# Products by halves: when the next down weights are loaded and cast, which low parts VectorE makes, and one piece of VectorE's order in the second feed-forward stage

## The chip, the cores and the metric

The kernel runs on one core of a Trainium2 chip. The metric is the device time of one execution in microseconds (us). A difference of about 0.5% (4.1 us here) is the least that a measurement of this kernel tells from no change.

## The reference

One encoder layer on 512 tokens of width 1024, all in float32: a feed-forward half-step, a mixer (Fourier groups beside grouped-query attention), a second feed-forward half-step, and a last norm.

```python
for _ in range(DEPTH):                                   # DEPTH = 1
    x = x + 0.5 * swiglu(rms_norm(x, ffn1_norm), ffn1_w_gate, ffn1_w_up, ffn1_w_down)
    h = rms_norm(x, mix_norm)
    u = h @ w_in
    ...
    x = x + jnp.concatenate([f_out, a_out], axis=-1) @ w_out
    x = x + 0.5 * swiglu(rms_norm(x, ffn2_norm), ffn2_w_gate, ffn2_w_up, ffn2_w_down)
return rms_norm(x, final_norm)

def swiglu(h, w_gate, w_up, w_down):
    return (jax.nn.silu(h @ w_gate) * (h @ w_up)) @ w_down
```

The feed-forward width is 2752: 21 blocks of 128 columns and a tail of 64. The change touches the two feed-forward stages alone.

## The kernel before

**Precision.** Each float32 operand of a product is split into a high part (a cast to fp32r, made by ScalarE) and a low part (source minus high part). A product is three TensorE passes: high by high, high by low, low by high. The low part is made in one of two ways: by a VectorE subtraction (`lows`, line 140), or by `rest_by_dma` (lines 169 and 170): ScalarE writes minus the high part into the place of the low part (an ACTIVATE), and GpSimd starts a DMA that adds the source to it.

**Stages.** Stage 1 (the first feed-forward, 0 to 330 us of the profile), the mixer (330 to 484 us), stage 2 (the second feed-forward, 484 us to the end). `ffn` makes both feed-forward stages.

**Groups.** Within a stage the 21 blocks j of the hidden width come in four groups. Stage 1: blocks 0, the tail "t", 1 and 2; then 3 to 8; 9 to 14; 15 to 20. Stage 2: blocks 0, "t" and 1; then 2 to 7; 8 to 13; 14 to 20. For each group the kernel multiplies the group's hidden activations by the group's part of the down weights: eight output tiles dn_0 to dn_7, each 128 by 512, three passes for each block of the group (18 matmuls for a group of six). The result of dn_d is added to the residual `gx` by VectorE (line 629). The first group's gate and up products are plain; the last of its plain pairs (block 2) is evacuated by `evacuate`, run from `rest()`.

**Products by halves.** The gate and up products of all later blocks are made by `seven`: the pair (gate, up) of a block is one 2 by 2 block product in seven half-size products instead of eight. One block takes one period of seven products, P0 to P5 and P9, of eight matmuls each. While group g's down products are made, the pairs for the next group are not yet under way: `seven` runs ahead of the down products of its group, over the blocks of that group but shifted by one (for the group 3 to 8 it makes blocks 4 to 9, six periods; the last loop of stage 1 makes 16 to 20, of stage 2 15 to 20). The last block's P9 and what hangs on it (the names in `LATE`) come after dn_0, by `rest()`.

**The order in a period** is written out in `TABLE`: names that end in h are ScalarE casts of weights, in l the low parts (a for the raw weights a11 and a12, s and t for their sums, d for a22), c1 to c4 the VectorE sums, f, g, p, l, u, v, si, mu, h the evacuation (pA: ScalarE copies half of bank q; pB, lA, lB, uA, uB: VectorE adds), nh or l the low part of the activation. A + or - moves a name to the next or the last block. ScalarE, VectorE and GpSimd follow this order inside `seven`; TensorE and SyncE follow the order of the program's text throughout; in the rest of `ffn` a list scheduler orders the other engines, with `issue_after` edges (`behind`) that put an instruction behind an anchor on the same engine.

**The places that the change touches.** `load_below()` starts the transfers of the raw down weights for dn_0 and dn_1 (`raw_tile`, line 164, on SyncE's queue). `below()` casts them (line 182) and makes their low parts (line 140); the two calls hang on the names in `BELOW`, at a block beyond the last. Raw down weights and raw up weights share three buffers ("raw"), so that a transfer starts when an earlier tile's last reader is done. A down weight's high and low part take two of the four shared slots of `ring`; dn_2 gets dn_0's slots, dn_3 gets dn_1's. In the last period of a group the low part of the last block's activation is made by VectorE, all others by `rest_by_dma`.

**What else a reader needs.** The first product of a period, P0, multiplies a11, whose low part is made by `rest_by_dma` (BY_DMA), so the transfer written `ring<-raw_g` has to land before P0's second matmul (line 452).

Of the kernel before, what the change touches and what calls it, by code (L numbers as in the profile page):

```python
# [12 lines left out]
ALU = mybir.AluOpType  # L13
# [26 lines left out]
PLACES = 7  # L40
HALF = S // 2
USES = "a11", "a12", "s2", "s1", "s4", "s3", "a22"
BELOW = 'a.h', 'd.h'
HELD = 2
FIRST = ("ld", "a.h", "a.l", "c1", "d.h", "d.l", "c2", "c3", "c4", "s.h", "s.l", "t.h", "t.l")
TABLE = """
# [47 lines left out]
def asf(ap):  # L94
    return ap.bitcast(F32)
# [3 lines left out]
def encoder(ctx, tc, A, out):  # L99
    nc = tc.nc  # L100
# [36 lines left out]
            f(*a)  # L137

    def lows(lo, src, hi):
        nc.vector.tensor_tensor(out=lo, in0=src, in1=asf(hi), op=ALU.subtract)  # L140

    def slot_at(tile, i, rooms=0):
        o = i * KD * P + rooms * ROOM
# [150 lines left out]
    def ffn(norm, after, wgu, wd, wdt, groups, opening, closing):  # L294
# [4 lines left out]
        n_ = norm.n  # L299
        n_plain = len(groups[0])  # L300
        with tc.tile_pool(name=f"act{n_}", bufs=1) as ap, tc.tile_pool(name=f"sums{n_}", bufs=2) as sp:
            room(ap, 128)
            acts = ap.tile([P, PLACES * 2 * S + ROOM], F32R, name=f"at{n_}")
            at = acts[:, FRONT + LOWER : FRONT + LOWER + PLACES * 2 * S].rearrange("p (n a b) -> p n a b", a=2, b=S)
# [5 lines left out]
            def place(j):  # L310
                where[j] = free.pop(0)
                return where[j]
# [8 lines left out]
            def gate(c, between={}, by_dma=False):  # L321
                with ExitStack() as behind:
                    for i in (norm.squared, norm.added) if n_ and c else ():
                        behind.enter_context(tc.issue_after(i.ins))
                    whi, wlo = weights(wgu[c], f"gu{n_}_{c}", by_dma=by_dma)
                ps = bank(f"gu{n_}_{c}")
                for k in range(KD):
                    between.get(k, int)()
                    product(ps, whi[:, k, :], wlo[:, k, :], hh[k], hl[k], k == 0, k == KD - 1, turn=True)
                return ps  # L330
# [38 lines left out]
            def back(ts):  # L369
                plain[:] = [t for t in plain if all(t is not q for q in ts)]  # L370
# [67 lines left out]
            anchors = {}  # L438

            def seven(js, first, finish, load_below, below):  # L440
# [86 lines left out]
                def do(i, name):  # L527
                    shift = name.count("+") - name.count("-")
                    name = name.rstrip("+-")
                    i += shift  # L530
                    if i == len(js) - 2 and name == "P3":
                        load_below()
                    if i == len(js) and name in BELOW:
                        below()
                    if i not in range(len(js)):
                        return
                    o = state.setdefault(i, {})
                    if "w" not in o:
                        o.update(prepare(js[i]))
                    if "P0" not in o:  # L540
                        o.update(evacuation(js[i], o))
                    if i and (i, name) != (1, "ld") or not i and name not in FIRST:
                        o["l" if name == "nh" and i == len(js) - 1 else name]()
                    if i == 0 and name == "P0":
                        finish()

# [12 lines left out]
            def down_raw(d, group, gi):  # L559

                js = [j for j in group if j != "t"]
                return raw_tile(wd[d][:, js[0] : js[-1] + 1, :], f"dn{n_}_{d}_{gi}", len(js))

            def down(d, group, gi):

                js = [j for j in group if j != "t"]
                src, halves_ = wd[d][:, js[0] : js[-1] + 1, :], closing and gi == len(groups) - 1 and d >= KD - LAST
                raw = raws[d] = loads.pop(0) if loads else down_raw(d, group, gi)
                whi, wlo = weights(src, "", len(js), raw, skip=SKIP if halves_ else 0)
                if halves_:  # L570
                    token_weights(d, js)
                w = wt[d // 4][:, d % 4 * P : (d % 4 + 1) * P]

                def steps(ps, t):
                    for i, j in enumerate(group):
                        h, l = (at[:, where[j], o, t] for o in range(2))
                        first, last = i == 0, i == len(group) - 1
                        turn = t == every
                        if j == "t":
                            o, h, l = (turned(p) if turn else p for p in (ps[:, t], h, l))  # L580
                            nc.tensor.matmul(o, w, h, start=first, stop=False)
                            nc.tensor.matmul(o, w, l, start=False, stop=last)
                        else:
                            k = j - js[0]
                            cut = first and d == KD - LAST and t == slice(0, HALF)
                            product(ps[:, t], whi[:, k, :], wlo[:, k, :], h, l, first, last, cut, turn)
                        yield

                return steps
# [44 lines left out]
            for gi, group in enumerate(groups):  # L634
                last = gi == len(groups) - 1
                ahead = []
                if gi:
                    downs, loads = [], []
                    rest = seven(
                        range(group[0] + 1, min(group[-1] + 2, NF)), ready, finish,  # L640
                        lambda: loads.extend(down_raw(d, group, gi) for d in range(2)),
                        lambda: downs.append(down(len(downs), group, gi)),
                    )
                else:
                    downs, loads = [], []
                    lent = [acts[:, FRONT + i * KD * P : FRONT + (i + 1) * KD * P] for i in range(PLACES - 4, PLACES)]
                    plain.extend(lent)
                    row = []
                    pss = dict(enumerate(opening(gate, lambda: norm.column([norm.acc]), lambda: row.append(norm.row()))))
                    back(lent[:2])  # L650
                    due, parts, left = [*pss, "t"], list(range(KH)), range(2 * len(pss), 2 * n_plain)
                    pss["t"] = [gate(2 * NF)]
                    tail_weights()
                    for i, c in enumerate(left):
                        pss.setdefault(c // 2, []).append(gate(c, by_dma=i in (1,) if n_ else i > 0))
                        if due:
                            j = due.pop(0)
                            evacuate(at[:, place(j)], n_, pss[j], norm)
                        if c % 2 and c != left[-1]:
                            due.append(c // 2)  # L660
                        while len(parts) * len(left) > (len(left) - 1 - i) * KH:
                            o = parts.pop(0)
                            operands(row[0], o, o + 1)

                    def rest():
                        evacuate(at[:, place(n_plain - 1)], n_, pss[n_plain - 1], norm)

                def added(d, ps):
                    residual(d, ps, every)
# [6 lines left out]
                for d in range(KD):  # L676
# [19 lines left out]
                    if d == 0:  # L696
                        rest()
                        if last:

                            lent = slots[KD - 2 : KD]  # L700
                            plain[0:0] = lent
                            continue
                    def finish(waiting=waiting, added=added if last or d < KD - 1 else lambda d, ps: residual(d, ps, every)):
                        for d_, ps, steps in waiting:
                            for _ in steps:
                                pass
                            added(d_, ps)
# [10 lines left out]
    def evacuate(at, n_, pss, norm):  # L718
        g = tp.tile([P, S], F32, tag="g", name=f"g{n_}p")
        u = tp.tile([P, S], F32, tag="u", name=f"u{n_}p")  # L720
        h, l = at[:, 0], at[:, 1]
        if len(pss) == 2:
            nc.vector.tensor_tensor(out=g, in0=pss[0], in1=norm.rb, op=ALU.mult)
            nc.vector.tensor_tensor(out=u, in0=pss[1], in1=norm.rb, op=ALU.mult)
            nc.scalar.activation(g, g, AF.Silu)
            nc.vector.tensor_tensor(out=u, in0=g, in1=u, op=ALU.mult)
            nc.scalar.copy(h, u)
            lows(l, u, h)
        else:

            o, p = slice(FT, P), slice(0, FT)
            nc.vector.tensor_tensor(out=u, in0=pss[0], in1=norm.rb, op=ALU.mult)
            nc.scalar.activation(g[o], u[p], AF.Silu)
            nc.vector.tensor_tensor(out=u[o], in0=g[o], in1=u[o], op=ALU.mult)
            nc.scalar.copy(h[o], u[o])
            nc.scalar.copy(h[p], u[o])
            lows(l[o], u[o], h[o])
            nc.scalar.copy(l[p], asf(l[o]))
# [909 lines left out]
```

## Time and profile before

| what | us |
|---|---|
| median of 3 runs | 822.95 (819.89 to 823.01) |
| the profiled execution's own time | 820.42 |
| its span, first to last instruction | 818.6 |
| TensorE busy with matmuls | 807.9 (99%) |
| VectorE, ScalarE, GpSimd busy | 639.8, 548.6, 83.5 |
| mean granted TensorE clock | 0.999 |

Rows of the timeline give start, length, engine, line, operation, out<-in (buffer numbers left out) and shapes; in brackets stands the engine's idle time ahead of the instruction and what ended it. SPq is SyncE's queue, PEld TensorE's weight load. A matmul's length holds its way through the array, so a stall is read from starts: back to back, matmuls of 512 columns start 0.22 us apart, and a pair of 512 and 256 columns takes 0.33 us. Rows of the DMA view give the transfers issued in a window: KB each and the time to landing. Rows of the waits view give the total, the number and the longest.

### The profile page before, as it was taken

To read this page: it belongs to the slowest core of one execution; us is meant where nothing else is said; L and a number is where in the kernel's file an instruction comes from. 1 tells how busy PE (TensorE), PEld (TensorE's weight loads), DVE (VectorE), ACT (ScalarE), POOL (GpSimd) and SP (SyncE) were. 2 spreads that over 40 slices of the span, in tenths; PEclk is the share of its full clock that TensorE was granted. 3 is DMA by queue.
4 is the path that set the end of the run, shared out by engine and by line. 5 is a ranking of instruction groups with operands and counts; after the bars stand their busy time and mean duration, and the time that the engine had idled before them with its cause. 6 is when DMAs were issued, how large, how long until landed. Compare 5 with 4: busy or idle time off the path is not lost.

```text
span 818.6 us, 11867 instructions
## 1 busy us (share of the span) xinstructions
PE 807.9 (99%) x4376; PEld 705.8 (86%) x4376; DVE 639.8 (78%) x1071; ACT 548.6 (67%) x876; POOL 83.5 (10%) x95
## 2 busy tenths in 40 slices
PE   9999999999999999999999999999999999999997
PEld 7888988898888888889988888889888988888886
DVE  7996998388856967799998588989874998389673
ACT  7774885278725845779999558568733875278562
POOL 0120210011100100211000001102100110011001
PEclk9999999999999999999999999999999999999999
DMA  7775885559644743352110325668653785459422
GB/s 258 178 166 158 192 208 135 147 141 215 141 160 96 175 102 116 104 174 78 52 53 26 103 67 146 150 199 202 170 141 103 182 208 135 151 130 216 97 77 104
DMA packets 40779, 115.82 MB, mean 141 GB/s; under 512 B 4752, under 2 KB 10256, under 8 KB 40720
## 3 DMA queue, kind: packets, MB, share of 16 engines
q1 hardware_dynamic: 27776, 82.61, 33.0%
q0 software_dynamic: 12224, 31.47, 20.7%
q10 hardware_dynamic: 720, 0.98, 0.3%
q8 instruction: 34, 0.56, 0.3%
q14 instruction: 25, 0.20, 0.1%
HBM read 84.24 MB, written 2.10 MB: 105 GB/s over the span
## 4 chain that ended last, share of the span: by engine, by line
PE 85%; DMA 9%; DVE 4%; issue 1%; ACT 1%; POOLq 0%; POOL 0%; DVEq 0%; ACTq 0%
PE dn L196 25%; PE r L449 12%; PE mix L196 9%; DMA ring<-raw_g 7%; PE r L452 7%; PE gu L196 3%; PE c L449 3%; PE p L449 3%; PE q L449 3%; PE gu L804 3%; PE mix L1304 2%; PE mix L1264 2%; PE c L452 2%; PE p L452 2%; PE q L452 2%
## 5 line engine op out<-in xcount | busy, mean ns | idle before, releaser
L196 PE MATMUL dn<-at,ring 128*128 128x512 f32 x900 | 203.4, 380 | 0.0
L196 PEld LDWEIGHTS dn<-at,ring 128*128 128x128 f32 x900 | 167.7, 188 | 29.0 <-DVE ring L140 0.2
L449 PE MATMUL r<-rt,ring 128*128 128x512 f32 x560 | 191.4, 383 | 0.0
L452 PE MATMUL r<-rt,ring 128*128 128x256 f32 x560 | 153.7, 274 | 3.2 <-DMA ring<-raw_g 3.2
L449 PEld LDWEIGHTS r<-rt,ring 128*128 128x128 f32 x560 | 105.1, 188 | 18.7
L452 PEld LDWEIGHTS r<-rt,ring 128*128 128x128 f32 x560 | 105.2, 188 | 5.5 <-DMA ring<-raw_g 5.1
L629 DVE SCALAR_TENSOR_TENSOR gx<-dn,gx 128x512 f32<-128x512 f32 x61 | 41.9, 690 | 76.4 <-PE dn L196 76.3
L182 ACT CAST ring<-raw_dn 128x768 fp32r<-128x768 f32 (+3 forms) x58 | 45.2, 783 | 67.0 <-PE dn L196 48.5
L140 DVE TENSOR_TENSOR ring<-s,ring 128x1024 fp32r<-128x1024 f32 x70 | 85.1, 1220 | 2.5 <-ACT ring L404 0.5
L404 ACT CAST ring<-s 128x1024 fp32r<-128x1024 f32 x70 | 72.6, 1043 | 6.0 <-PE p L449 5.6
L140 DVE TENSOR_TENSOR ring<-raw_dn,ring 128x768 fp32r<-128x768 f32 (+3 forms) x58 | 51.6, 893 | 6.2 <-issue 4.1
L170 POOL DMA_DIRECT2D ring<-raw_g x35 | 30.0, 858 | 249.1 <-ACT ring L169 179.5
L169 ACT ACTIVATE ring<-ring 128x1024 fp32r<-128x1024 f32 x38 | 40.3, 1060 | 13.6 <-PE dn L196 12.5
L196 PE MATMUL gu<-ring 128*128 128x512 f32 x216 | 48.9, 381 | 0.0
L449 PE MATMUL c<-rt,ring 128*128 128x512 f32 x140 | 48.6, 383 | 0.0
L449 PE MATMUL p<-rt,ring 128*128 128x512 f32 x140 | 48.5, 383 | 0.0
L449 PE MATMUL q<-rt,ring 128*128 128x512 f32 x140 | 48.4, 382 | 0.0
L485 ACT COPY p<-r 128x512 f32<-128x512 f32 x35 | 19.9, 570 | 41.9 <-PE r L452 41.9
L196 PEld LDWEIGHTS gu<-ring 128*128 128x128 f32 x216 | 40.4, 188 | 6.9
L170 POOL DMA_DIRECT2D at<-u x29 | 24.9, 858 | 200.1 <-ACT p L505 192.0
L404 ACT CAST ring<-raw_g 128x1024 fp32r<-128x1024 f32 x35 | 36.8, 1051 | 11.9 <-DMA raw_g<-in_wgu 11.9
L452 PE MATMUL c<-rt,ring 128*128 128x256 f32 x140 | 38.4, 274 | 0.0
(282 smaller groups left out, 1704.8 us busy)
## 6 DMA issues: line engine op xcount, KB each, us to landing
raw_g<-in_wgu SPq DMA_DIRECT2D x35, 512.0 KB, 4.2
raw_u<-in_wgu SPq DMA_DIRECT2D x35, 512.0 KB, 5.4
ring<-raw_g POOLq DMA_DIRECT2D x35, 512.0 KB, 7.6
raw_dn<-in_wd SPq DMA_DIRECT2D x40, 384.0 KB, 3.3
at<-u POOLq DMA_DIRECT2D x29, 256.0 KB, 3.8
raw_gu<-in_wgu SPq DMA_DIRECT2D x12, 512.0 KB, 3.8
raw_o<-in_wo SPq DMA_DIRECT2D x8, 512.0 KB, 3.4
raw_dn<-in_wd SPq DMA_DIRECT2D x8, 448.0 KB, 3.7
```

The source lines that it names most:

```text
L140: nc.vector.tensor_tensor(out=lo, in0=src, in1=asf(hi), op=ALU.subtract)
L169: nc.scalar.activation(lo, asf(hi), AF.Copy, scale=-1.0)
L170: nc.gpsimd.dma_start(out=lo, in_=src, accum_op=ALU.add)
L182: nc.scalar.copy(hi[:, :n, :], raw[:, :n, :])
L196: nc.tensor.matmul(ps, a, b, start=first and b is mhi and a is whi, stop=last and a is wlo)
L404: nc.scalar.copy(hi, src())
L449: nc.tensor.matmul(turned(ps), whi[:, ks], turned(m), start=first and i == 0, stop=False, skip_group_check=True)
L452: nc.tensor.matmul(turned(ps[:, :HALF]), wlo[:, ks], turned(m[:, :HALF]), start=False, stop=i == KH - 1, skip_group_check=True,)
L485: nc.scalar.copy(o[key], o["r"])
L629: nc.vector.scalar_tensor_tensor(out=x[d][:, t], in0=ps[:, t], scalar=0.5, in1=x[d][:, t], op0=ALU.mult, op1=ALU.add)
L804: nc.tensor.matmul(turned(pss[c]), w[:, k % 2, c], turned(m[k]), start=k == 0 and m is hh and w is hi, stop=k == KD - 1 and w is lo,)
L1264: nc.tensor.transpose(pts[n][:, c * P : (c + 1) * P], prob[t, b, c][:, kc * P : (kc + 1) * P], ident)
```

## The change

Four edits, none of which alters what is computed.

1. `load_below()` is called at P0 of a loop's last block, no longer at P3 of the block before.
2. `below()` hangs on "c3" and "t.h", no longer on "a.h" and "d.h": dn_0's cast and low part move behind pA of the last period, dn_1's to where a further period's t.h would stand, behind the last block's Silu.
3. In the last group of a stage, the low part of the last block but one is made by VectorE too (the others of that group stay with the DMA). One ScalarE ACTIVATE and one GpSimd DMA go, one VectorE subtraction of 128 by 512 comes, in each stage.
4. In stage 2 the subtraction at the end of the last plain pair's evacuation becomes the VectorE anchor: what `behind` emits from then on (the down weights' low parts and the sums c1 to c4 of the first pair by halves, block 3) stands behind it on VectorE.

```diff
-BELOW = 'a.h', 'd.h'
+BELOW = "t.h", "c3"
...
     def lows(lo, src, hi):
-        nc.vector.tensor_tensor(out=lo, in0=src, in1=asf(hi), op=ALU.subtract)
+        return nc.vector.tensor_tensor(out=lo, in0=src, in1=asf(hi), op=ALU.subtract)
...
-                    if i == len(js) - 2 and name == "P3":
+                    if i == len(js) - 1 and name == "P0":
                         load_below()
                     if i == len(js) and name in BELOW:
                         below()
...
-                        o["l" if name == "nh" and i == len(js) - 1 else name]()
+                        o["l" if name == "nh" and i >= len(js) - 1 - last else name]()
...
                     def rest():
-                        evacuate(at[:, place(n_plain - 1)], n_, pss[n_plain - 1], norm)
+                        done = evacuate(at[:, place(n_plain - 1)], n_, pss[n_plain - 1], norm)
+                        if n_:
+                            anchors["DVE"] = done
...
-            lows(l, u, h)
+            return lows(l, u, h)
```

TensorE's list of instructions is the same, row by row. Three places where instructions stand differently, or where one might expect them to:

**SyncE's queue at the end of the loop over blocks 4 to 9 (stage 1).** raw_g and raw_u are a block's raw weights, raw_dn_d those of dn_d; in brackets stand the semaphores that are waited for. Before:

```order
L393 DMA raw_g_9_1047<-in_wgu 128x1024 [waits DMASW1_49,DMAHW1_49,DVE_49,Activation_49]
L393 DMA raw_u_9_1048<-in_wgu 128x1024 [waits DMAHW0_49]
L164 DMA raw_dn_0_1_1146<-in_wd 128x768 [waits DMAHW2_49,Activation_49]
L164 DMA raw_dn_1_1_1148<-in_wd 128x768 [waits DMAHW4_49,DVE_49,Activation_49]
L393 DMA raw_g_10_1332<-in_wgu 128x1024 [waits DMAHW3_49,DMASW3_49,DVE_49]
L393 DMA raw_u_10_1333<-in_wgu 128x1024 [waits DMAHW6_49,DVE_49,Activation_49]
L164 DMA raw_dn_2_1_1337<-in_wd 128x768 [waits DMAHW7_49,DVE_49]
```

The same place with the change:

```order
L393 DMA raw_g_9_1047<-in_wgu 128x1024 [waits DMASW1_49,DMAHW1_49,DVE_49,Activation_49]
L393 DMA raw_u_9_1048<-in_wgu 128x1024 [waits DMAHW0_49]
L164 DMA raw_dn_0_1_1185<-in_wd 128x768 [waits DMAHW2_49,Activation_49]
L164 DMA raw_dn_1_1_1187<-in_wd 128x768 [waits DMAHW4_49,DVE_49,Activation_49]
L393 DMA raw_g_10_1332<-in_wgu 128x1024 [waits DMAHW3_49,DMASW3_49,DVE_49]
L393 DMA raw_u_10_1333<-in_wgu 128x1024 [waits DMAHW6_49,DVE_49,Activation_49]
L164 DMA raw_dn_2_1_1337<-in_wd 128x768 [waits DMAHW7_49,DVE_49]
```

Nothing moved: between the two places of the call no other transfer is issued on SyncE's queue, and the transfers for dn_0 and dn_1 wait for the same readers of the same buffers (the cast of block 7's and of block 8's raw up weights).

**VectorE at the end of the same loop.** The names are those of `TABLE`'s tiles: s the sums and their low parts, g, p, u the evacuation's tiles of the block numbered. Before:

```order
L140 TENSOR_TENSOR ring<-raw_dn_0_1_1146,ring 128x768
L140 TENSOR_TENSOR ring<-s_0_9_1116,ring 128x1024
L459 TENSOR_TENSOR u_8_1185<-u_8_1185,r_8_1090 128x256
L140 TENSOR_TENSOR ring<-raw_dn_1_1_1148,ring 128x768
L514 TENSOR_TENSOR u_8_1185<-g_8_1139,u_8_1185 128x512
L140 TENSOR_TENSOR ring<-s_0_9_1172,ring 128x1024
L459 TENSOR_TENSOR g_9_1235<-g_9_1235,p_9_1201 128x256
L459 TENSOR_TENSOR p_9_1261<-p_9_1261,q_9_1242 128x256
L459 TENSOR_TENSOR g_9_1235<-c_9_1237,p_9_1261 128x256
```

With the change, from the second-last of these on:

```order
L459 TENSOR_TENSOR g_9_1231<-g_9_1231,p_9_1199 128x256
L140 TENSOR_TENSOR ring<-raw_dn_0_1_1185,ring 128x768
L459 TENSOR_TENSOR p_9_1257<-p_9_1257,q_9_1238 128x256
L459 TENSOR_TENSOR g_9_1231<-c_9_1233,p_9_1257 128x256
L459 TENSOR_TENSOR u_9_1271<-r_9_1189,p_9_1257 128x256
L459 TENSOR_TENSOR u_9_1271<-u_9_1271,r_9_1189 128x256
L459 TENSOR_TENSOR g_9_1231<-g_9_1231,c_9_1233 128x256
L419 TENSOR_TENSOR s_0_10_1411<-raw_u_10_1333 128x512
L140 TENSOR_TENSOR ring<-raw_u_10_1333,ring 128x512
L419 TENSOR_TENSOR s_0_10_1481<-raw_g_10_1332,raw_u_10_1333 128x512
L419 TENSOR_TENSOR s_0_10_1411<-s_0_10_1411,raw_g_10_1332 128x512
L140 TENSOR_TENSOR ring<-raw_dn_1_1_1187,ring 128x768
```

dn_0's low part now stands between gB and pB of the last block, dn_1's behind three more adds and four instructions for block 10. ScalarE at that place, with the change (before, raw_dn_0 and raw_dn_1 stood ahead of the two casts of s_0_9, nine rows further up):

```order
L505 COPY p_9_1257<-q_9_1238 128x256
L182 CAST ring<-raw_dn_0_1_1185 128x768
L404 CAST ring<-raw_g_10_1332 128x1024
L404 CAST ring<-raw_u_10_1333 128x512
L169 ACTIVATE ring<-ring 128x1024
L509 ACTIVATE g_9_1231<-g_9_1231 128x512
L182 CAST ring<-raw_dn_1_1_1187 128x768
L182 CAST ring<-raw_dn_2_1_1337 128x768
```

dn_0's cast is the first thing behind pA, dn_1's follows the last block's Silu (g_9), and dn_2's cast keeps its place behind them.

**VectorE at the opening of stage 2**, behind the first residual (u2p is block 2's activation, s_2_3 the sums of block 3). Before:

```order
L629 SCALAR_TENSOR_TENSOR gx<-dn_0_0_4917,gx 128x512
L140 TENSOR_TENSOR ring<-raw_dn_3_0_4948,ring 128x256
L419 TENSOR_TENSOR s_2_3_5024<-raw_u_3_4976 128x512
L419 TENSOR_TENSOR s_2_3_5043<-raw_g_3_4975,raw_u_3_4976 128x512
L140 TENSOR_TENSOR at_4612<-u2p,at_4612 128x512
L140 TENSOR_TENSOR ring<-raw_u_3_4976,ring 128x512
L419 TENSOR_TENSOR s_2_3_5024<-s_2_3_5024,raw_g_3_4975 128x512
L629 SCALAR_TENSOR_TENSOR gx<-dn_1_0_4947,gx 128x512
L140 TENSOR_TENSOR at_4612<-raw_dn_4_0_4962,at_4612 128x256
```

With the change:

```order
L629 SCALAR_TENSOR_TENSOR gx<-dn_0_0_4916,gx 128x512
L140 TENSOR_TENSOR at_4611<-u2p,at_4611 128x512
L140 TENSOR_TENSOR ring<-raw_dn_3_0_4947,ring 128x256
L419 TENSOR_TENSOR s_2_3_5023<-raw_u_3_4975 128x512
L419 TENSOR_TENSOR s_2_3_5042<-raw_g_3_4974,raw_u_3_4975 128x512
L140 TENSOR_TENSOR ring<-raw_u_3_4975,ring 128x512
L629 SCALAR_TENSOR_TENSOR gx<-dn_1_0_4946,gx 128x512
L140 TENSOR_TENSOR at_4611<-raw_dn_4_0_4961,at_4611 128x256
L419 TENSOR_TENSOR s_2_3_5023<-s_2_3_5023,raw_g_3_4974 128x512
```

The subtraction for u2p moved up by three rows, and the low part of dn_4 now has one block-3 sum fewer ahead of it (c2 follows it). Further down, the low part of dn_7 likewise moved ahead of block 3's last low part.

## The prediction

> **What bounds the kernel now.** I read the page's busy shares first, then the waits, then the timeline at each wait, TensorE first. The page's first part and the rows of the waits view for TensorE's two sides:
>
> ```profile
> PE 807.9 (99%) x4376; PEld 705.8 (86%) x4376; DVE 639.8 (78%) x1071; ACT 548.6 (67%) x876; POOL 83.5 (10%) x95
> PE r L452 <- DMA ring<-raw_g: 3.2, 6, 1.2
> PE dn L196 <- DVE at L140: 0.5, 1, 0.5
> PEld r L452 <- DMA ring<-raw_g: 5.1, 6, 1.5
> ```
>
> TensorE is the bound: of a span of 818.6 us it is idle for 818.6 - 807.9 = 10.7. No edit takes a matmul away, so the change can only win part of that, and it can lose wherever it makes TensorE wait anew. The named waits are two kinds: six at P0's second matmul, on the DMA that makes a11's low part (one before the last loop period of each of six loops; 3.2 us as TensorE's own idle time, 5.1 by its weight load), and one of 0.5 on VectorE at a down product. The first kind, in stage 1's first loop:
>
> ```profile
> 109.57 0.39 PE L449 MATMUL r<-rt,ring 128*128 128x512 f32 x1
> ...
> 110.12 0.38 PE L452 MATMUL r<-rt,ring 128*128 128x256 f32 x1 [0.16 <-DMA ring<-raw_g]
> ...
> 100.73 0.46 SPq L393 DMA_DIRECT2D raw_u<-in_wgu  x1
> 100.80 0.86 POOL L170 DMA_DIRECT2D ring<-raw_g  x1 [1.45 <-ACT ring L169]
> ...
> 101.30 0.37 SPq L164 DMA_DIRECT2D raw_dn<-in_wd  x1
> ```
>
> Starts 109.57 to 110.12 are 0.55 apart where a matmul of 512 columns takes 0.22: 0.33 lost. Within 0.6 us the accumulating DMA, a raw_u and a raw_dn start together. The DMA view of narrow windows shows how long each takes: first the accumulating DMA a period earlier (issued at 91.47), then the two issued at 100.80 and 101.30, then the raw_dn of another group's end (189.54), then raw_dn issued into quieter stretches (121.66 and 132.41):
>
> ```profile
> ring<-raw_g POOLq DMA_DIRECT2D x1, 512.0 KB, 7.7
> ring<-raw_g POOLq DMA_DIRECT2D x1, 512.0 KB, 9.3
> raw_dn<-in_wd SPq DMA_DIRECT2D x1, 384.0 KB, 8.9
> raw_dn<-in_wd SPq DMA_DIRECT2D x1, 384.0 KB, 10.0
> raw_dn<-in_wd SPq DMA_DIRECT2D x1, 384.0 KB, 3.2
> raw_dn<-in_wd SPq DMA_DIRECT2D x1, 384.0 KB, 4.0
> ```
>
> With raw_dn in company the accumulating DMA takes 9.3 instead of 7.7, 1.6 more than TensorE's slack there of about 1.3 (1.6 less the 0.33 lost). So this is where moving the transfer of raw_dn could win.
>
> **Edit 1, the call of load_below.** It would win that only if it moved the transfer. SyncE's list, shown ahead, is the same row for row, with the same waits, since no other transfer lies between the old place of the call and the new one, and raw_dn_0 waits only for the cast of block 7's raw_u, long done. Nothing holds it: it will still start about 0.5 us behind raw_u. Cost and gain 0; the six waits stay.
>
> **Edit 2, casts and low parts at the six group ends** (128.71, 217.98 and 297.09 in stage 1, three alike in stage 2). What moves costs no instruction; the question is whether dn_0's and dn_1's low parts come before TensorE's third matmul on each. The rows of the first group end (those of TensorE, ScalarE, VectorE and GpSimd that the walk uses):
>
> ```profile
> 126.56 0.36 ACT L505 COPY p<-q 128x256 f32<-128x256 f32 x1
> 126.81 1.05 ACT L404 CAST ring<-raw_g 128x1024 fp32r<-128x1024 f32 x1
> ...
> 128.71 1.06 PE L196 MATMUL dn<-at,ring 128*128 128x512 f32 x4
> ...
> 129.37 0.42 DVE L459 TENSOR_TENSOR u<-u,r 128x256 f32<-128x256 f32 x1
> 129.63 0.86 POOL L170 DMA_DIRECT2D ring<-raw_g  x1 [1.83 <-ACT ring L169]
> 129.70 0.41 DVE L459 TENSOR_TENSOR g<-g,c 128x256 f32<-128x256 f32 x1
> ...
> 130.03 0.68 DVE L419 TENSOR_TENSOR s<-raw_u 128x512 f32<-128x512 f32 x1
> 130.15 0.63 ACT L509 ACTIVATE g<-g 128x512 f32<-128x512 f32 x1 [0.81 <-DVE g L459]
> 130.64 0.69 DVE L140 TENSOR_TENSOR ring<-raw_u,ring 128x512 fp32r<-128x512 f32 x1
> ...
> 132.67 0.84 ACT L182 CAST ring<-raw_dn 128x768 fp32r<-128x768 f32 x1 [1.89 <-PE dn L196]
> ...
> 133.77 0.95 DVE L140 TENSOR_TENSOR ring<-raw_dn,ring 128x768 fp32r<-128x768 f32 x1
> ...
> 134.04 0.82 PE L196 MATMUL dn<-at,ring 128*128 128x512 f32 x3
> ```
>
> dn_0: its cast takes the slot behind pA's copy at 126.81 and ends 0.84 later, at 127.65; its low part then runs 127.68 to 128.63. The third matmul of dn_0 is due at 128.71 + 2 x 0.22 = 129.15: 0.5 to spare. dn_1: on VectorE pB follows at about 128.5 and four adds at 0.33 to 0.45 each, so the last add lB comes at 130.12 instead of 129.70; Silu follows at 130.57, dn_1's cast 131.1 to 131.95. Four block-10 instructions at 0.60 (130.03 to 130.64) from 130.45 put dn_1's low part at 132.86 to 133.81. It is due at 134.04 + 0.44 = 134.48: 0.67 to spare. Silu's 0.42 delay reaches no product: the activation waits for P9 anyway, which comes behind dn_0, and block 9's is first read by the next group. In the last groups no further block's sums follow; by the same walk dn_0's low part ends about 0.8 before need, and dn_1's about 1.1. So the term is 0. No gain is possible, since TensorE has no wait in these rows now (a matmul each 0.22 from 128.71 on); the upper bound takes a whole 0.95 more on VectorE ahead of dn_1's low part, less the 0.67 to spare, 0.3 at each of four ends: 1.2.
>
> The Trainium skill, "VectorE: DVE Perf Modes", section "The DRAIN you can't avoid", says that VectorE's next operation does not begin until the pipe is empty. The trace's operations of 0.69 start 0.60 apart, so it overlaps their ends. By the page the walk to dn_1 would be some 0.6 longer and the margin gone, a cost of 0 to 0.1 per group; by the row it is free, and the row decides.
>
> What is later for it: the raw buffers of dn_0 and dn_1 come free later, and dn_2's transfer (issued at 121.66 now) has to wait for dn_0's low part, to about 128.7. dn_2 begins at 134.04 + 18 x 0.22 = 138.0, its low part is needed at 138.0 + 0.44, so the transfer must land by 138.44 less 0.84, 0.95 and two hand-overs: 136.6. It may thus take 7.9 us; alone it took 3.2 and 4.0. raw_dn_3 and raw_dn_4 go out at 132.4 and 134, 10 us and more before their need. The accumulating DMA for block 10 starts 0.8 later (130.4 instead of 129.63), and is needed at about 160. Cost 0. GpSimd's other queue entries stand behind that one and are needed later still.
>
> By the Trainium skill, "DMA: Bandwidth & Descriptors", section "Anatomy of one DMA — SWDGE (gpsimd) path", a transfer costs about 2 us plus its bytes at 436 GB/s, which for 384 KB makes an estimate of 2.9 us. The row of 3.2 agrees for a lone transfer; the rows 8.9 and 10.0 do not, and by those the sum would be that of the second rival below.
>
> **Edit 3, the last block but one of a stage.** ScalarE loses one ACTIVATE (0.63), GpSimd one DMA, VectorE gains one subtraction of 0.69, twice in the program. No row of the waits has TensorE waiting for that transfer, so its end wins nothing. VectorE's row ahead of it is not full: in the last group it idles before its adds:
>
> ```profile
> 297.29 0.42 DVE L459 TENSOR_TENSOR u<-r,p 128x256 f32<-128x256 f32 x1 [0.91 <-PE r L452]
> ...
> 302.36 0.42 DVE L459 TENSOR_TENSOR u<-u,r 128x256 f32<-128x256 f32 x1 [3.00 <-ACT u L512]
> ```
>
> 0.91 and 3.00 us of idle time take the 0.69. Cost 0, counted in the bound above.
>
> **Edit 4, the opening of stage 2.** This is the only place where a wait of TensorE goes:
>
> ```profile
> 525.35 0.42 DVE L140 TENSOR_TENSOR ring<-raw_dn,ring 128x256 fp32r<-128x256 f32 x1
> 525.79 0.33 SPq L164 DMA_DIRECT2D raw_dn<-in_wd  x1
> ...
> 526.71 0.69 DVE L419 TENSOR_TENSOR s<-raw_u 128x512 f32<-128x512 f32 x1 [0.94 <-DMA raw_u<-in_wgu]
> ...
> 527.92 0.69 DVE L140 TENSOR_TENSOR at<-u2p,at 128x512 fp32r<-128x512 f32 x1
> ...
> 529.67 0.62 PE L196 MATMUL dn<-at 128*128 128x512 f32 x2
> ...
> 530.32 0.42 DVE L140 TENSOR_TENSOR at<-raw_dn,at 128x256 fp32r<-128x256 f32 x1
> ...
> 530.80 0.49 PE L196 MATMUL dn<-at 128*128 128x512 f32 x1 [0.51 <-DVE at L140]
> ...
> 531.13 0.39 PE L581 MATMUL dn<-at,wt 128*128 128x512 f32 x1
> ...
> 535.86 1.10 PE L196 MATMUL dn<-at 128*128 128x512 f32 x3
> ...
> 535.99 0.42 DVE L140 TENSOR_TENSOR at<-raw_dn,at 128x256 fp32r<-128x256 f32 x1
> ...
> 536.80 0.39 PE L449 MATMUL r<-rt,ring 128*128 128x512 f32 x1
> ```
>
> dn_4's third matmul was due at 529.67 + 0.44 = 530.11 and came at 530.80: 0.69 lost, and the next, at 531.13 instead of 531.02, 0.11 more. dn_7's three matmuls took 535.86 to 536.80, 0.94 instead of 0.66: 0.28 more, since its low part came at 535.99. Sum 1.08. Now u2p's subtraction moves into VectorE's idle 0.94 before 526.71 (525.73, then dn_3's low part at 526.34, done by 526.76), and c2 goes behind dn_4: two instructions of 0.60 each fewer ahead of dn_4's low part. From c1 at 526.71: 527.32, 527.92, 528.52 (the residual), then dn_4's low part 529.12 to 529.54, before 530.11. dn_7's stands ahead of the subtraction of 1.22 and ends at about 534.9, before 535.50. Gain 1.08. Against it: raw_dn_5 starts once dn_3's low part is done, 1.0 later than its 525.79. The quiet row of 3.2 and the 4.0 are for three times its bytes; were it 0.4 late for dn_5, 0.7 would be left. Bounds 0.7 and 1.08; I take 1.08, as a transfer of a third of the 384 KB should not take longer than those.
>
> **Sum.** 0 + 0 + 0 - 1.08: span 817.5, and with 1.8 around it an execution of 819.3. The profiled execution, 820.42, stands at 2.5 below the median shown (822.95) and inside its runs (819.89 to 823.01); 1.1 off the median gives 821.9.
>
> **Rivals.** First, the transfers do move, or the crowd at P0 thins: the six waits (5.1 by the weight load's row, the larger of the two) go too: 821.9 - 5.1 = 816.8. For it stands only the pairing of 9.3 and 7.7; against it that SyncE's list and waits are the same. Second, slower: dn_2's transfer, now started at 128.7, shares the engines with raw_u and the accumulating DMA (issued at 130.4) as those of 8.9 and 10.0 did. It then lands at 137.6 or 138.7, 1.0 or 2.1 past 136.6, at each of four ends: 4.1 or 8.4 less 1.08, 826.0 or 830.3. It decides from a transfer of 7.9 us on. Against it: the accumulating DMA issued at 129.63 with raw_dn at 132.41 beside it left that at 4.0. Third, the opening's gain is eaten: 0.4 on dn_5 and up to 1.2 at the group ends, 822.5 to 823.
>
> **Numbers.** Forecast 0.81, first rival 0.06, second 0.06, third 0.07. A measurement of this kernel can tell about 0.5%, 4.1 us, from no change: faster means below 818.8 and slower above 827.1. Faster: the first rival, and a twentieth of the forecast, whose run medians may fall with the lower of the runs shown: 0.10. Slower: half the second rival and a little for an unknown: 0.05. Same: 0.85. The range takes the spread of the runs shown, about 3 us downward and 1 to 3 upward with the third rival: 818.0 to 825.0.
>
> **What would show it.** Right: raw_dn_0's issue still 0.5 us behind raw_u, six waits of "r L452" on the accumulating DMA of about 3.2 us, no row of a down product waiting for "at L140" at stage 2's opening, and its dn_4 in 0.22 steps. Wrong: a TensorE wait for raw_dn, ScalarE or VectorE behind 128.71 and its like; raw_dn_2 in flight for more than 7.9 us; or the six waits gone.

## The result and the profile after

| | before | the change |
|---|---|---|
| median of 20 runs, us | 821.17 | 820.09 |
| ratio to before, with its 95% interval | | 0.9984 (0.9977 to 0.9992) |
| profiled execution, us | 820.42 | 820.24 |
| its span, us | 818.6 | 818.5 |

One of the 20 runs of the change took 1568.43 us at a granted clock of 0.831; the ratio leaves it out, and the median of the other 19 is 820.06.

By the bound of 0.5% this is no change; by the interval it is a small gain, 0.7 to 1.9 us (1.08 between the medians). TensorE's busy row and its waits, in the page's first part and the waits view of the change:

```profile
PE 807.1 (99%) x4376; PEld 706.0 (86%) x4376; DVE 640.1 (78%) x1073; ACT 548.8 (67%) x874; POOL 81.8 (10%) x93
...
PE r L452 <- DMA ring<-raw_g: 4.4, 6, 1.2
PE busy L751 <- PEq L1633: 0.8, 1, 0.8
PE gu L806 <- ACT ring L792: 0.3, 1, 0.3
```

The row "PE dn L196 <- DVE at L140" is gone, and there is no row of a down product at a group end. The six waits at P0 are all there, and in this execution they are 1.2 us longer than in the one of before (4.4 against 3.2), about as much as the change gains elsewhere, so the two spans look alike.

The opening of stage 2 begins with dn_0's first matmul, in the timeline of before and then of the change:

```profile
522.63 0.38 PE L196 MATMUL dn<-at,ring 128*128 128x512 f32 x1
```

```profile
523.59 0.38 PE L196 MATMUL dn<-at,ring 128*128 128x512 f32 x1
```

Further on in the change (VectorE's low parts of u2p, dn_4 and dn_7, TensorE's products):

```profile
526.71 0.69 DVE L140 TENSOR_TENSOR at<-u2p,at 128x512 fp32r<-128x512 f32 x1 [0.38 <-ACT at L729]
...
529.97 0.82 PE L196 MATMUL dn<-at,ring 128*128 128x512 f32 x3
530.06 0.41 DVE L140 TENSOR_TENSOR at<-raw_dn,at 128x256 fp32r<-128x256 f32 x1
...
530.63 0.82 PE L196 MATMUL dn<-at 128*128 128x512 f32 x3
...
535.52 0.41 DVE L140 TENSOR_TENSOR at<-raw_dn,at 128x256 fp32r<-128x256 f32 x1
535.91 0.82 PE L196 MATMUL dn<-at 128*128 128x512 f32 x3
536.57 0.39 PE L449 MATMUL r<-rt,ring 128*128 128x512 f32 x1
```

dn_4's three matmuls now stand together at 530.63 and take 0.82 like any three; before, the third came 1.13 behind the first. From dn_7's first matmul to block 3's P0 it is 536.57 - 535.91 = 0.66, three pitches of 0.22; before it was 0.94. From dn_0's first matmul to block 3's P0 it is 536.57 - 523.59 = 12.98, and before it was 536.80 - 522.63 = 14.17: 1.19 us less in this pair of profiles. Everything here stands about 0.95 later than before; 0.73 of that is the longer waits at P0 in stage 1.

The first group end, in the same timeline, and SyncE's queue a period and a half ahead of it:

```profile
128.29 0.96 DVE L140 TENSOR_TENSOR ring<-raw_dn,ring 128x768 fp32r<-128x768 f32 x1 [2.44 <-ACT ring L182]
129.28 0.33 SPq L164 DMA_DIRECT2D raw_dn<-in_wd  x1
129.30 0.38 PE L196 MATMUL dn<-at,ring 128*128 128x512 f32 x1
...
133.56 0.95 DVE L140 TENSOR_TENSOR ring<-raw_dn,ring 128x768 fp32r<-128x768 f32 x1
134.64 0.38 PE L196 MATMUL dn<-at,ring 128*128 128x512 f32 x1
```

```profile
100.98 0.46 SPq L393 DMA_DIRECT2D raw_u<-in_wgu  x1
101.55 7.27 SPq L164 DMA_DIRECT2D raw_dn<-in_wd  x2
```

dn_0's low part ends at 129.25, 0.5 ahead of the third matmul (129.30 + 0.44 = 129.74). The transfer of raw_dn_0 starts 0.57 behind raw_u's, as before: the new place of the call moved nothing.

### The profile page after: what moved, and what is told of

Read it like the earlier page. It is cut to its first block, busy times and chain, and to the rows that moved or that the text cites. A ratio compares the mean times of both kernels' runs of the same rounds, so it can differ in the third digit from the quotient of the medians.

```text
span 818.5 us, 11871 instructions
## 1 busy us (share of the span) xinstructions
PE 807.1 (99%) x4376; PEld 706.0 (86%) x4376; DVE 640.1 (78%) x1073; ACT 548.8 (67%) x874; POOL 81.8 (10%) x93
## 4 chain that ended last, share of the span: by engine, by line
PE 90%; DMA 8%; issue 0%; DVE 0%; ACT 0%; POOLq 0%; POOL 0%; DVEq 0%
PE dn L196 25%; PE r L449 12%; PE mix L196 9%; PE gu L196 8%; DMA ring<-raw_g 7%; PE r L452 7%; PE p L449 3%; PE c L449 3%; PE q L449 3%; PE gu L806 3%; PE mix L1306 2%; PE mix L1266 2%; PE p L452 2%; PE q L452 2%; PE c L452 2%; PE mix L1104 1%
## 5 line engine op out<-in xcount | busy, mean ns | idle before, releaser
L196 PE MATMUL dn<-at,ring 128*128 128x512 f32 x900 | 203.3, 380 | 0.0
L196 PEld LDWEIGHTS dn<-at,ring 128*128 128x128 f32 x900 | 167.6, 188 | 28.8
L140 DVE TENSOR_TENSOR ring<-s,ring 128x1024 fp32r<-128x1024 f32 x70 | 85.3, 1219 | 2.5 <-ACT ring L404 0.6
L140 DVE TENSOR_TENSOR ring<-raw_dn,ring 128x768 fp32r<-128x768 f32 (+3 forms) x58 | 51.6, 892 | 14.7 <-ACT ring L182 13.7
L196 PE MATMUL gu<-ring 128*128 128x512 f32 x216 | 48.9, 381 | 0.0
L196 PEld LDWEIGHTS gu<-ring 128*128 128x128 f32 x216 | 40.4, 188 | 6.9
L404 ACT CAST ring<-raw_g 128x1024 fp32r<-128x1024 f32 x35 | 36.8, 1050 | 10.3 <-DMA raw_g<-in_wgu 10.3
L170 POOL DMA_DIRECT2D at<-u x27 | 23.2, 858 | 185.0 <-ACT p L505 185.0
L459 DVE TENSOR_TENSOR u<-u,r 128x256 f32<-128x256 f32 x70 | 29.4, 421 | 13.1 <-ACT u L512 11.9
```

Source lines behind the costliest of these rows:

```text
L140: return nc.vector.tensor_tensor(out=lo, in0=src, in1=asf(hi), op=ALU.subtract)
L170: nc.gpsimd.dma_start(out=lo, in_=src, accum_op=ALU.add)
L196: nc.tensor.matmul(ps, a, b, start=first and b is mhi and a is whi, stop=last and a is wlo)
L404: nc.scalar.copy(hi, src())
L459: return nc.vector.tensor_tensor(out=out, in0=a, in1=b, op=ALU.add)
```

## The experiments

All ratios are to the kernel before, run on the same chip beside the experiment.

### Which edit carries the gain

**Edit 4 alone.** The kernel before with the return value of `lows` and `evacuate` and

```diff
-                        evacuate(at[:, place(n_plain - 1)], n_, pss[n_plain - 1], norm)
+                        done = evacuate(at[:, place(n_plain - 1)], n_, pss[n_plain - 1], norm)
+                        if n_:
+                            anchors["DVE"] = done
```

> Edit 4 alone (stage 2's opening), all else as before. Theory (the forecast's): it carries the whole gain, ratio to before about 0.9987 (1.08 us less), and TensorE's row of a down product waiting for 'at L140' is gone. Rival (the gain comes from edits 1 to 3): ratio 1.000 and the row stays.

Measured: 820.68 us, ratio 0.9989 (0.9978 to 0.9999). TensorE's waits:

```profile
PE r L452 <- DMA ring<-raw_g: 3.1, 5, 1.2
PE busy L751 <- PEq L1633: 0.8, 1, 0.8
PE gu L806 <- ACT ring L792: 0.2, 1, 0.2
```

The row at stage 2's opening is gone, as the theory has it, and from dn_0's first matmul to block 3's P0 it is 12.98 us as with the whole change.

**Edits 1 to 3 without edit 4.** The change without the two lines `if n_:` and `anchors["DVE"] = done`.

> Edits 1 to 3 without edit 4. Theory: nothing at the group ends costs or wins, ratio 1.000 within 0.0010; no row of TensorE waiting at the six group ends, and the 0.5 us row at stage 2's opening is back. Rival (edits 1 to 3 lengthen the six waits at P0, which in the one profile of the change sum to 4.4 us instead of 3.2): ratio 1.0015, six waits at 4.4 again.

Measured: 821.62 us, ratio 1.0005 (0.9995 to 1.0015). The six waits sum to 4.3:

```profile
PE r L452 <- DMA ring<-raw_g: 4.3, 5, 1.5
```

By time edits 1 to 3 are worth nothing within 0.15%, but 4.3 is what the rival said. That called for the pieces apart. One thing did not come as expected: TensorE's row at stage 2's opening is not back. What is back is a smaller loss: the opening takes 13.56 us there, against 12.98 with edit 4. Without edit 4 the opening is 13.56 to 14.18 in five profiles (before, edit 1 alone, edit 3 alone, edits 1 and 2, edits 1 to 3); with it, 12.98 in the two profiles of the change and in that of edit 4 alone. So edit 4 saves 0.6 to 1.2 us, by how long the opening happened to take without it.

**Edits 1 and 2 alone, and edit 3 alone.**

```diff
-BELOW = 'a.h', 'd.h'
+BELOW = "t.h", "c3"
...
-                    if i == len(js) - 2 and name == "P3":
+                    if i == len(js) - 1 and name == "P0":
```

> Edits 1 and 2 alone (call of load_below, places of the casts and low parts). Theory: no time, ratio 1.000 within 0.0010, no row of TensorE waiting for down weights at the group ends; and the length of the six waits at P0 differs from execution to execution (3.2 before, 3.1 with edit 4 alone, 4.4 with the change, 4.3 without edit 4), so that here it is anywhere from 3.0 to 4.5. Rival (edits 1 and 2 lengthen the six waits): 4.3 or more, ratio 1.0015.

```diff
-                        o["l" if name == "nh" and i == len(js) - 1 else name]()
+                        o["l" if name == "nh" and i >= len(js) - 1 - last else name]()
```

> Edit 3 alone (low part of the last block but one of a stage by VectorE). Theory: no time, ratio 1.000 within 0.0010, six waits anywhere from 3.0 to 4.5. Rival (edit 3 is what lengthens them): 4.3 or more here and about 3.2 with edits 1 and 2 alone, ratio 1.0015.

Measured: 821.05 us and 0.9994 (0.9985 to 1.0003) with edits 1 and 2; 821.06 us and 0.9993 (0.9984 to 1.0002) with edit 3. Neither is told from no change. The waits with edits 1 and 2:

```profile
PE r L452 <- DMA ring<-raw_g: 4.6, 4, 1.5
...
PE dn L196 <- DVE at L140: 0.2, 1, 0.2
```

and with edit 3:

```profile
PE r L452 <- DMA ring<-raw_g: 3.1, 5, 1.3
...
PE dn L196 <- DVE at L140: 0.5, 1, 0.5
```

**Edit 1 alone, and the change once more.**

> Edit 1 alone: the call of load_below at its new place, everything else as before. Theory: the program is the one of before, instruction by instruction, so 820 to 823 us and the six waits as in any execution of before. The length of the six waits has been 3.2, 3.1 and 3.1 us in profiles without edits 1 and 2 and 4.4, 4.3 and 4.6 with both; if the split is of edits 1 and 2, it is about 3.1 here.

> The change once more, for a second profile. If edits 1 and 2 lengthen the six waits, they sum to 4.3 or more again; if the length is the execution's, 3.0 to 4.6.

With edit 1 alone every engine's list of instructions in the trace is that of before; it took 820.46 us, and the change 819.94, one run each. The waits were 2.8 and 3.4:

```profile
PE r L452 <- DMA ring<-raw_g: 2.8, 5, 1.3
```

```profile
PE r L452 <- DMA ring<-raw_g: 3.4, 4, 1.3
```

So the waits sum to 2.8 to 3.2 in four profiles without edit 2 and to 3.4 to 4.6 in four with it. The view lists four to six of the six, since it leaves out the shortest. Taken from starts (P0's second matmul behind its first, less 0.22), all six lose 3.9 to 4.3 us without edit 2 and 4.5 to 5.8 with it. In the change's own two profiles they lose 5.4 and 4.5, so a good part of any such difference is the execution's. The first loop's wait shows the same: all that edit 2 moves comes after it (ScalarE's list first differs at 117.48), and still it ranges from 0.18 to 0.68 over the eight.

That the two sets don't overlap points to a cost of edit 2, 1.1 us by the means of the starts, most of it in stage 1's second and third loops (1.5 to 1.9 us together without edit 2, 2.2 to 3.2 with it). The ratios do not show it: 0.9994 (at most 1.0003) with edits 1 and 2, 1.0005 with edits 1 to 3, and 0.9984 for the change against 0.9989 for edit 4 alone. It stays open.

### Whether the margin at the group ends was real

The change with dn_0's low part five adds later on VectorE:

```diff
-BELOW = "t.h", "c3"
+BELOW = "t.h", "s.h"
```

> The change with dn_0's cast and low part hung on s.h instead of c3: ScalarE's place stays behind pA, VectorE's low part goes behind lB, the last of the five adds, at all six group ends. By the walk of the prediction the low part then starts at 130.03 instead of 127.68 at the first group end and ends at 130.98, where dn_0's third matmul is due at 129.15: TensorE waits 1.9 us at each of six ends, 11.4 together, ratio to before 1.011 to 1.014 (830 to 832 us). That would show that the 0.5 us to spare was a real bound. Rival (the due time is later than the walk has it, the low part is read late in the tile): under 3 us together, ratio under 1.004.

Measured: 832.1 us, ratio 1.0123 (1.009 to 1.0156). The waits view, and TensorE and VectorE at the first group end in the timeline:

```profile
PE dn L196 <- DVE ring L140: 10.4, 6, 1.9
```

```profile
129.35 0.62 PE L196 MATMUL dn<-at,ring 128*128 128x512 f32 x2
...
130.67 0.95 DVE L140 TENSOR_TENSOR ring<-raw_dn,ring 128x768 fp32r<-128x768 f32 x1
...
131.68 0.49 PE L196 MATMUL dn<-at,ring 128*128 128x512 f32 x1 [1.71 <-DVE ring L140]
```

Two matmuls go out, and the third waits for the low part: 131.68 - 129.35 = 2.33 where two pitches are 0.44, so 1.89 is lost, against 1.9 from the walk. Six ends make 11.3, and the median stands 10.5 above that of before and 12.0 above that of the change. The low part is read where the walk had it, so the 0.5 us to spare was the whole margin.

### What the first rival would have given

The transfers of raw_dn_0 and raw_dn_1 put where `load_below` stands in the program, by issuing them on ScalarE's queue, which inside `seven` keeps the order of the text (`queue` is passed on to `raw_tile`):

```diff
-        nc.sync.dma_start(out=raw[:, :n, :], in_=src)
+        (queue or nc.sync).dma_start(out=raw[:, :n, :], in_=src)
...
-                        lambda: loads.extend(down_raw(d, group, gi) for d in range(2)),
+                        lambda: loads.extend(down_raw(d, group, gi, nc.scalar) for d in range(2)),
```

> The change, but the transfers of raw_dn_0 and raw_dn_1 of the six loops are issued on ScalarE's queue at load_below's place in the program, behind pA of the block before (about 118 in the first loop instead of 101 and 108). Theory: SyncE's running ahead is what kept the transfers where they were, and raw_dn in flight is what makes the accumulating DMA late; so the latter lands in 7.4 to 7.7 us instead of 9.3 to 10.3, the six waits (3.2 to 4.4 us in TensorE's row) go to below 1, and the ratio to before is 0.993 to 0.996 (816 to 818 us). Rival: raw_u in the same stretch is enough to make it late; the six waits stay above 2.5 us and the ratio is 0.998 to 0.999. Further rival: dn_0's cast now waits for its transfer and TensorE waits at the group ends: ratio above 0.999.

Measured: 815.48 us, ratio 0.9934 (0.992 to 0.9948). The transfers' issue in the timeline, and the waits:

```profile
116.38 0.33 ACTq L164 DMA_DIRECT2D raw_dn<-in_wd  x1
...
116.75 1.48 ACTq L164 DMA_DIRECT2D raw_dn<-in_wd  x1
```

```profile
PE r L452 <- DMA ring<-raw_g: 0.8, 3, 0.4
```

Three of the six waits are gone and the rest is 0.8 us. So the mechanism of the first rival is right, and its condition (the transfers move) is what the change does not meet. The prediction priced it at 5.1 us; 0.9934 against the change's 0.9984 is 4.1. The accumulating DMA lands in 7.8 us in the first loop and 9.3 in the second, later than the 7.4 to 7.7 expected, which is why three waits are left.

**The same without the change's other edits:** the kernel before with the late transfers at the old place of the call, and then with edit 4 too.

> The kernel before, with the same two transfers issued on ScalarE's queue at load_below's old place (behind the cast of block 7's activation, about 116.7), casts and low parts in their old places. Theory: the six waits go as in the run with the change, but dn_0's cast, due at 117.5, waits some 3 us for its transfer on ScalarE, and the casts of the sums behind it come as much later; the sums' slack is about 1 to 2 us, so TensorE loses 0 to 2 us at each loop: ratio 0.995 to 1.006, and worse than the run with the change by 0.001 or more. That would show what edit 2 is worth once the transfers are really later. Rival (edit 2 is not needed for it): the same ratio as the run with the change within 0.0008.

> The kernel before with the late transfers on ScalarE's queue and edit 4, without edits 1 to 3. Theory after the first four runs: the late transfers take 3.6 us from before and edit 4 another 1.1 to 1.6, so 816.0 to 816.5, ratio 0.9937 to 0.9944, equal to the change with late transfers (0.9934) within its interval: the later casts of edit 2 are worth 0 to 0.8 us. Rival (edit 2 is needed once transfers are late): 0.9955 or more, with TensorE waits at the group ends.

Measured: 817.59 us, ratio 0.9957 (0.9942 to 0.9971), and with edit 4 817.3 us, 0.9939 (0.9925 to 0.9952). In the first, dn_0's cast waits for its transfer, 1.18 us rather than the 3 expected:

```profile
118.27 0.84 ACT L182 CAST ring<-raw_dn 128x768 fp32r<-128x768 f32 x1 [1.18 <-DMA raw_dn<-in_wd]
```

and TensorE's waits show nothing that follows from it:

```profile
PE r L452 <- DMA ring<-raw_g: 1.1, 3, 0.4
PE dn L196 <- DVE at L140: 1.0, 1, 1.0
```

The second row is stage 2's opening, twice as long here as before; edit 4 takes it away. So edit 4 is part of what sets the first of these runs behind the change with late transfers, and not edit 2 alone. With edit 4 the ratio is that of the change with late transfers (0.9934) within either interval. The later casts of edit 2 are therefore not needed for late transfers as far as these intervals (each about 0.14% to either side) can tell, and no cost of theirs shows either.

### What else stands beside the accumulating DMA

raw_u of a loop's later blocks issued on ScalarE's queue behind the cast t.h, some 3.5 us after the accumulating DMA starts, first with the late raw_dn and then without:

```diff
-P0 a.h+ ... P1 d.h+ mu- t.h d.l+ ...
+P0 a.h+ ... P1 d.h+ mu- t.h lu++ d.l+ ...
...
+                def load_u(queue=nc.scalar):
+                    t["u"] = wp.tile([P, KD * P], F32, tag="raw", name=f"raw_u{n_}_{j}")
+                    queue.dma_start(out=t["u"].rearrange("p (a b) -> p a b", b=P), in_=wgu[2 * j + 1])
...
+                    if name == "ld" and i > 1:
+                        name = "lg"
+                    if name == "lu" and i < 2:
+                        return
```

> The change with the late transfers on ScalarE's queue, and the transfers of raw_u in the loops (from the third block of a loop on) later too, on ScalarE's queue behind the cast t.h, some 4 us behind the accumulating DMA's start. Theory (what makes the accumulating DMA late is what shares the engines with it): it lands in 6 to 7 us instead of 7.5 to 9.3, the three waits that are left (0.8 us in TensorE's row, 1.3 to 1.6 by starts) go, ratio to before 0.9915 to 0.993. Rival (raw_u is now itself late for its casts, or holds up the next accumulating DMA): a new TensorE wait, ratio 0.994 or more.

> The change with the late raw_u alone; raw_dn_0 and raw_dn_1 on SyncE's queue as in the change, so that raw_dn_0 starts behind raw_g beside the accumulating DMA. Theory (any second transfer beside the accumulating DMA costs about the same): it lands in 8 to 9.3 us as with raw_u alone in company, the six waits are 0.5 to 1.7, ratio to before 0.993 to 0.996, near the late transfers of raw_dn alone (0.9934). Rival (only raw_dn matters, its rows are shorter): the waits stay above 2.5, ratio above 0.997.

Measured: 813.85 us, ratio 0.9904 (0.9891 to 0.9918), with both late, the fastest of all; and 815.86 us, 0.9926 (0.9901 to 0.9951), with raw_u late alone. Both ratios lie a little below what was expected (0.9915 and 0.993 at the least), by less than their intervals tell. With both late, TensorE's waits have no row of P0 left:

```profile
PE busy L761 <- PEq L1643: 0.8, 1, 0.8
PE gu L816 <- ACT ring L802: 0.4, 1, 0.4
```

with raw_u late alone there are two waits:

```profile
PE r L458 <- DMA ring<-raw_g: 1.1, 2, 0.6
```

How long the accumulating DMA for the block after the first loop's block 7 takes (issued at 100.7 to 101.1), in the DMA view of the change, of late raw_dn, of late raw_u, and of both:

```profile
ring<-raw_g POOLq DMA_DIRECT2D x1, 512.0 KB, 9.6
```

```profile
ring<-raw_g POOLq DMA_DIRECT2D x1, 512.0 KB, 7.8
```

```profile
ring<-raw_g POOLq DMA_DIRECT2D x1, 512.0 KB, 7.5
```

```profile
ring<-raw_g POOLq DMA_DIRECT2D x1, 512.0 KB, 5.8
```

In this loop each of the two transfers that doesn't start beside it is worth 1.7 to 2.1 us to it. P0 needs it after about 9 (issue 100.80, P0's second matmul due at 109.79), so here either one is enough. In the second loop the figures differ: it takes 10.3 in the change, 9.3 with late raw_dn, 9.6 with late raw_u (8 to 9.3 was expected) and 7.0 with both. One alone is worth 0.7 to 1.0 there, the second 2.3 to 2.6 more, and only both end the wait.

The Trainium skill, "DMA: Bandwidth & Descriptors", section "Rules for kernel authors", says that spreading transfers over several issuing engines gives no bandwidth, since all run on the same 16 DMA engines and interleave. No run here tests that by itself: each late transfer changed its queue and its start together, and a move to ScalarE's queue at the old time was not tried. That the start matters without a change of queue is seen in the kernel before: its accumulating DMA for block 10, issued at 129.63 with the next transfer on SyncE's queue only at 132.41, took 5.1 us. The same section's advice to issue a transfer early is what raw_dn and raw_u run against: each could start later (by about 15 and 3.5 us in the first loop) without a new wait at P0, and the wait that they made was up to 1.2 us long in the profiles of before and of the change.

## Why the prediction was right, point by point

- **The bound.** Right: with the change's own edits these two kinds of wait are the ones that moved, and nothing else gave or took more than the intervals show.
- **Edit 1, nothing moves.** Right, by the list of instructions and by raw_dn's issue 0.57 behind raw_u's.
- **Edit 2, free at the group ends.** Right in the trace of the change: low part of dn_0 at 127.68 to 128.63 in the old time, 128.29 to 129.25 in one that is 0.59 later; dn_1's at 132.86, measured 133.56, 0.11 later than that shift. In stage 1's last group dn_0's low part ends 0.8 before need as forecast (297.63 against 298.44), dn_1's 2.6 and not 1.1 (300.47 against 303.12). Pushing dn_0's by five adds cost 1.89 a time against 1.9. The sentence drawn from the Trainium skill, "VectorE: DVE Perf Modes", section "The DRAIN you can't avoid", would have made the walk longer; the trace decided, and the section itself excepts an operation that nothing holds.
- **dn_2's transfer (the second rival).** It went out at 129.28, which is the 128.7 of the walk in the shifted time, and took 3.2 us of the 7.9 that were free. The rival falls. (The prediction's estimate of 2.9 us for a lone transfer uses a figure that its section gives for transfers issued by GpSimd; raw_dn is issued by SyncE.)
- **Edit 3, free.** Right: 0.9993 (0.9984 to 1.0002).
- **Edit 4, 1.08 us.** Right in mechanism and size. In the pair of profiles the opening is 1.19 us shorter; alone the edit has 0.9989 (0.1 to 1.8 us). dn_4's low part starts at 530.06, where the forecast's 529.12 stands in a time 0.95 later. The upper bound was the right end: no product of dn_5 waits in the change. That the medians differ by 1.08, the forecast to the digit, is luck: their interval is 0.7 to 1.9, and the opening of before takes 13.56 to 14.18 from one profile to another. One detail differs: u2p's low part was to fill VectorE's idle 0.94; in the shifted time it came when forecast, but it waited 0.38 for ScalarE's cast ahead of it.
- **Third rival** (gain eaten at group ends): edits 1 to 3 measure 1.0005 (0.9995 to 1.0015), and TensorE's rows show no wait for down weights at a group end. Nothing of its 1.2 us shows there; whether edit 2 adds to the six waits, which no rival of the prediction had, stays open. By its own terms (0.4 and up to 1.2 on top of 821.9) this rival's range is 822.3 to 823.5, wider than the 822.5 to 823 given.
- **The mis-sized term.** The median: 821.9 was forecast from 822.95, the middle of three runs of before. Twenty runs have 821.17, so the level was 1.8 lower than taken, and 820.09 came out. The difference was right, its starting point was not.
- **The span**, forecast 817.5, was 818.5 in the profile, because six waits of 3.2 became 4.4 in that execution (3.4 in the next). Their spread from one execution to the next was left out of the forecast for a single profile.

## What to carry to other kernels

The place of a call in the text sets when a transfer starts only if something on its queue holds it there; on a queue that runs ahead, read the neighbours and the semaphores, and if the transfer has to start later, issue it from an engine whose order is busy with the work that it should follow. A transfer that starts before it has to is not free when it starts beside one that the bound engine waits for: here starting two kinds of them later took the ratio from the change's 0.9984 to 0.9904. And an instruction may be moved late until the first matmul that reads its result, not just until the first matmul of that tile: here a walk with measured pitches gave the cost of missing that point to within 0.1 us.

## What the runs showed that was not expected

- An accumulating DMA of 512 KB took 5.8, 7.5 to 8.0 and 9.1 to 9.6 us with one, two and three plain transfers started within 0.7 us of it (the first loop in all profiles). In the second loop, with the same transfers started near it, it took 7.0, 9.0 to 9.6 and 9.4 to 10.7. Between the four profiles of the last experiment one more costs 0.7 to 2.6 us, and not the same in each loop.
- dn_0's cast, with its transfer issued only 2.0 us ahead of its turn (115.06), waited 1.18 us on ScalarE, and no product noticed.
- The six waits of the same program differ by 1.0 us in sum from one profile to the next, about as much as the whole change is worth; a single pair of profiles would have shown a gain of 0.1 us in span.
